# Zero products in TensorE's waits, placed by a new build-time estimate

## The chip, the cores and the metric

One core of one Trainium2 chip. The metric is device time in microseconds of one launch of the whole program; lower is better.

## The reference

Two networks one after the other, 256 latent tokens of width 1024 beside 256 context tokens, batch 1, all in float32. The first has two layers. Each applies a gated feed-forward (`swiglu`, hidden 2816), a mixer and a second feed-forward, every one behind a root-mean-square norm whose gain, shift and output gate come from a conditioning vector through a large matrix (`ada_w`). The mixer of layer 0 is a gated delta rule in both directions (8 heads of 128); that of layer 1 is windowed attention with sinks (16 heads of 64, 4 for keys and values). The second network takes the 256 latent tokens and has two layers too: each a mixer (a gated linear recurrence beside causal latent attention with rotary positions, 16 heads, mixed by gates), a layer norm, a feed-forward with a convolution of three taps over time, and a layer norm:

```
x = first_block(x, c, ctx, ...)
for l in range(2):
    x = layer_norm(ALPHA * x + mixer_sublayer(x, ...))
    x = layer_norm(ALPHA * x + conv_ffn(x, w_up[l], ..., w_down[l]))
```

## The kernel before

Activations lie transposed, features in the 128 partitions and tokens in the free dimension, as 8 blocks for width 1024. Large weights come through one queue (SyncE) in pieces of 128 x 1024 float32, in the fixed order of `pieces()` (line 209). Each float32 weight is split by `convert` and `lower` (lines 464, 482) into a high part h, rounded to TensorE's faster float32r form, and a remainder lo = w − h; activations are split in the same way. A product is then three float32r matmuls (`mm3`, line 518): high by high, high by low, low by high. Products of the first network's feed-forwards have 512 columns (context and latent tokens), those of the last 256 columns only latent tokens. Attention, norms' sums, recurrences and the delta rule use plain float32 products.

All instructions are written by one Python program at build time; nothing reorders them later. `Ker` holds a list of threads (generators), each a step of the network, with a priority. A thread yields what it needs next (`need`, line 325: tiles that must be written, free buffers, keys). `run` (line 337) picks the next thread: the first by priority whose needs are estimated to be ready by the time that TensorE gets free, else the one ready soonest. Readiness comes from an estimate: every instruction passes through `note` (line 278), which adds a cost by engine, size and type to that engine's clock (`self.clock`) and writes down when the tile is written (`self.wrote`) and read (`self.read`). All dependencies of `note` go by whole tiles. So the estimate sets the order in which every engine gets its work; each engine then runs its own list in that order and waits by semaphores.

Two more choices use the clocks. `flex` (line 402) gives a subtraction, product or sum of two SBUF operands to VectorE or to GpSimd, whichever is estimated to end first; `lower` and the second half of every split go through it. `copy` (line 409) and `affine` (line 416) choose between ScalarE and VectorE.

The places where one stage hands over to the next: `norm_half` (line 812) for the first network's norms, each half of the tokens by itself, and `layer_norm` (line 1810) for the second network. Both sum squares by products with ones (128 columns of output), take a power on GpSimd, spread the result over the partitions by a second set of products, and then normalise the eight blocks one by one on VectorE and ScalarE; `linear2` (line 537) consumes these blocks as they come, two weight pieces at a time. The delta rule's inner solve (`dn_join`, line 1238) uses many products of 16 to 64 rows.

Of the kernel before, what the change touches and what calls it, by code (L numbers as in the profile page):

```python
# [8 lines left out]
F32 = mybir.dt.float32  # L9
F32R = mybir.dt.float32r  # L10
BF16 = mybir.dt.bfloat16
I32 = mybir.dt.int32
AF = mybir.ActivationFunctionType
ALU = mybir.AluOpType
AX = mybir.AxisListType

P = 128
# [100 lines left out]
def pack_w(w):  # L118

    import numpy as np  # L120

    k, n = w.shape
    return np.ascontiguousarray(w.reshape(k // P, P, n // P, P).transpose(2, 1, 0, 3)).reshape(n // P, P, k)


def layouts(a):
# [29 lines left out]
    wo = a["dn_w_out"][0]  # L156
    we = wo[:P * EARLY, :768].reshape(EARLY // 2, 2, P, 2, 384)
    o["dn_oe"] = np.ascontiguousarray(we.transpose(3, 0, 2, 1, 4)).reshape(EARLY, P, 768)
    o["dn_ol"] = np.ascontiguousarray(wo[P * EARLY:, :768]).reshape(8 - EARLY, P, 768)
    o["dn_out"] = pack_w(wo[:, 768:])  # L160
# [48 lines left out]
def pieces():  # L209
# [7 lines left out]
    o += t("dn_in", [8 * s + h for w, h in DN_ORDER for s in {"k": (1,), "q": (0, 2), "z": (3,)}[w]])  # L217
    o += t("dn_oe", range(EARLY)) + t("dn_ol", range(8 - EARLY)) + t("dn_out", range(2))
    o += weave(w1(0, 1) + w2(0, 1), ada(0, 8) + ada(1, 0, 1, 2))
# [11 lines left out]
class Engine:  # L231
# [5 lines left out]
    def __getattr__(self, op):  # L237
        fn = getattr(self.real, op)

        def call(*a, **k):  # L240
            self.K.note(self.name, op, a, k)
            return fn(*a, **k)  # L242

        setattr(self, op, call)
        return call
# [8 lines left out]
NBLK, NRAW, NHL, NSM = 70, 5, 4, 22  # L254


class Ker:
    def __init__(self, ctx, tc, I, out):
        self.tc, self.I, self.out = tc, I, out
        self.nc = Engines(self, tc.nc)  # L260
        pool = lambda n, b, **k: ctx.enter_context(tc.tile_pool(name=n, bufs=b, **k))
        self.keep = pool("keep", 1)
        self.pools = {
            "r": (pool("raw", NRAW), NRAW), "w": (pool("hl", NHL), NHL), "b": (pool("blk", NBLK), NBLK),
            "s": (pool("sm", NSM), NSM), "p": (pool("ps", 8, space=bass.MemoryType.PSUM), 8),
        }
        self.live = {k: set() for k in self.pools}
        self.dr = pool("dr", 3, space=bass.MemoryType.DRAM)
        self.n = 0
        self.clock = {n: 0.0 for n in ("tensor", "vector", "scalar", "gpsimd", "sync", "dma")}  # L270
        self.wrote, self.read = {}, {}
        self.threads, self.done = [], set()
        self.order, self.at, self.loaded = pieces(), 0, 0
        self.dm, self.cv, self.ahead = [], [], NRAW - 2
        self.most, self.lag, self.low = NHL, False, None


    def note(self, eng, op, a, k):
        aps = [x for x in a if isinstance(x, bass.AP)]
        kin = [x for n, x in k.items() if isinstance(x, bass.AP) and n != "accum_out"]  # L280
        outs = aps[:1] + ([k["accum_out"]] if k.get("accum_out") is not None else [])
        ins = aps[1:] + kin
        o = aps[0]
        n = math.prod(o.shape[1:])
        cols = sum(1 for x in ins if math.prod(x.shape[1:]) == 1)
        if eng == "tensor":
            if op == "matmul":
                m = aps[2]
                n = math.prod(m.shape[1:])
                c = n * {F32: 1.68, BF16: 0.44}.get(m.dtype, 0.422)  # L290
                if m.dtype == F32 and o.shape[0] <= 64:
                    c *= o.shape[0] / P
            else:
                c = 109.0
        elif eng == "scalar":
            c = 75 + 0.83 * n + 93 * cols + (93 if len(outs) > 1 else 0)
        elif eng == "vector":
            fast = op in ("tensor_copy", "tensor_scalar", "memset") and not any(x.space == bass.MemoryType.PSUM for x in ins)
            c = 65 + n * (6.6 if op == "reciprocal" else 0.52 if fast else 1.04) + 60 * cols
        elif eng == "gpsimd":  # L300
            c = 60 + n * (165 if ALU.pow in a else 2.28 if op == "tensor_tensor" else 1.5)
        else:
            c = 450
        key = lambda x: x.tensor.name
        t = self.clock[eng]
        for x in ins:
            e, w = self.wrote.get(key(x), (0.0, eng))
            t = max(t, e + (200 if w != eng or eng != "tensor" else 0))
        for x in outs:
            for table in (self.wrote, self.read):  # L310
                e, w = table.get(key(x), (0.0, eng))
                if w != eng:
                    t = max(t, e + 200)
        t += c
        self.clock[eng] = t
        if eng == "sync":
            b = math.prod(o.shape) * 4
            self.clock["dma"] = t = max(self.clock["dma"], t) + b / 340
            t += 1700
        for x in ins:  # L320
            self.read[key(x)] = (max(t, self.read.get(key(x), (0.0, ""))[0]), eng)
        for x in outs:
            self.wrote[key(x)] = (t, eng)

    def need(self, *aps, b=0, p=0, s=0, when=None, e=None):

# [10 lines left out]
    def run(self):  # L337

        while self.threads:
            best = None  # L340
            for th in self.threads:
                aps, b, p, s, when, e = th[3]
                if (when and not when()) or b > self.free_of("b") or p > self.free_of("p") or s > self.free_of("s"):
                    continue
                r = max([self.wrote[x.tensor.name][0] + 200 for x in aps], default=0.0)
                if e:
                    r = max(r, self.clock[e] - SLACK)
                if best is None or r < best[0]:
                    best = (r, th)
                if r <= self.clock["tensor"]:  # L350
                    break
            assert best, ("no thread can go on", [(t[0], t[2], t[3][1:]) for t in self.threads], {k: len(v) for k, v in self.live.items()})
            th = best[1]
            try:
                th[3] = next(th[2]) or self.need()
            except StopIteration:
                self.threads.remove(th)
# [6 lines left out]
    def get(self, kind, shape, dt=F32):  # L364
        pool, n = self.pools[kind]
        assert len(self.live[kind]) < n, (kind, sorted(self.live[kind]))
        t = pool.tile(list(shape), dt, tag=kind, name=self.nm(kind))
        self.live[kind].add(t.tensor.name)
        return t

    def free(self, *tiles):
        for t in tiles:
            for s in self.live.values():
                if t.tensor.name in s:
                    s.remove(t.tensor.name)
                    break
            else:
                raise AssertionError(t.tensor.name)

    def bank(self):  # L380
        return self.get("p", (P, 512))
# [20 lines left out]
    def flex(self, n):  # L402

        now = self.clock["tensor"]
        d = max(now, self.clock["vector"]) + 65 + 1.04 * n
        g = max(now, self.clock["gpsimd"]) + 60 + 2.28 * n
        return self.nc.vector if d <= g else self.nc.gpsimd

    def copy(self, out, x):
# [54 lines left out]
    def convert(self):  # L464

        while self.free_of("w") and len(self.cv) < self.most:
            e = next((e for e in self.dm if e[0][0] != "ada"), None)
            if e is None or (self.cv and self.wrote[e[1].tensor.name][0] > self.clock["tensor"] + 1000):
                return
            self.dm.remove(e)  # L470
            key, t, n = e
            w = self.get("w", (P, 2, 1024), F32R)
            h, lo = w[:, 0], w[:, 1]
            self.copy(h[:, :n], t[:, :n])
            self.lower()
            self.low = h[:, :n], lo[:, :n], t
            if not self.lag:
                self.lower()
            self.cv.append((key, h, lo))
            self.fill()  # L480
# [123 lines left out]
    def setup(self):  # L604
        nc, I = self.nc, self.I
        keep = lambda n, shape, dt=F32: self.keep.tile(list(shape), dt, name=n)
# [3 lines left out]
        o, w = PAR_COLS["cond"]  # L610
# [18 lines left out]
        self.fill()  # L629
        self.cbf = keep("cbf", (P, 384), BF16)  # L630
        nc.sync.dma_start(self.cbf, I["cbf"])
        self.row = keep("row", (P, 48))
        nc.sync.dma_start(self.row, I["row"])
        self.sel = keep("sel", (P, 4))
# [808 lines left out]
    def deltanet(self, X, i, segs, nxt):  # L1443
# [53 lines left out]
        for g in (0, 3):  # L1497
            B = []
            for j in range(EARLY // 2):
                W = yield from self.pull("dn_oe", 0, EARLY // 6 * g + j)  # L1500
                yield self.need(p=0 if B else 3)
# [747 lines left out]


EARLY = 6
FLIGHT = 4
ROOMQ = 6
SLACK = 1000
# [39 lines left out]
```

## Time and profile before

| | us |
|---|---|
| median of 3 runs | 2867.35 (2855.65 to 2868.4) |
| the profiled execution | 2863.03 |
| its span, first to last instruction | 2861.2 |
| TensorE busy | 2741.8 (96%) |
| VectorE busy | 2160.0 (75%) |
| ScalarE busy | 910.1 (32%) |
| GpSimd busy | 675.9 (24%) |
| mean granted TensorE clock | 0.977 of full |

Busy shares are averages over the whole span. PE stands for TensorE's matmuls, PEld for its weight loads, DVE for VectorE, ACT for ScalarE, POOL for GpSimd, SP for SyncE. Because every instruction goes through one helper, almost all have the line L242; groups are told apart by tile names (p a PSUM bank, w a split weight, r a raw weight, b a block of activations, s a small tile, io the identity and ones). A matmul's duration includes its way through the array, so neighbours overlap; how fast they follow each other is read from their count in a window. [...]

### The profile page before, as it was taken

How to read it: one execution, taken by the hardware profiler on the slowest of the kernel's cores; microseconds unless marked ns; L12 is line 12 of the kernel's file. 1: busy time of each engine (PE TensorE's matmuls, PEld its weight loads, DVE VectorE, ACT ScalarE, POOL GpSimd, SP SyncE). 2: the span in 40 equal slices, each digit the busy share in tenths (PEclk: the TensorE clock that was granted, in tenths of full speed). 3: DMA queues.
4: the chain of work that ended last, by engine and by line, in shares of the span. 5: the costliest groups of instructions: out<-in, count | busy, mean ns of one | idle time of the engine just before them, and what ended most of it. 6: DMA issues, size and time to landing. Idle time of an engine off the chain costs nothing.

```text
span 2861.2 us, 47754 instructions
## 1 busy us (share of the span) xinstructions
PE 2741.8 (96%) x18916; PEld 2448.6 (86%) x18916; DVE 2160.0 (75%) x3980; ACT 910.1 (32%) x1980; POOL 675.9 (24%) x680
## 2 busy tenths in 40 slices
PE   7999999999989999999999999999899999898998
PEld 5888888888878888888888968999888999888998
DVE  5898868677756777668766578876878986878995
ACT  3111126345422110021111254214654333753432
POOL 3000335335412000120001322103513323512230
PEclk9999999999999999999999999999999999999999
DMA  7666542112223555536666213655434655334653
GB/s 268 196 186 205 182 148 78 46 39 74 61 71 114 182 154 179 152 109 200 186 209 187 79 60 93 190 179 170 144 113 142 186 174 166 116 113 132 197 171 118
DMA packets 145120, 412.59 MB, mean 144 GB/s; under 512 B 31232, under 2 KB 38144, under 8 KB 144896
## 3 DMA queue, kind: packets, MB, share of 16 engines
q1 hardware_dynamic: 144896, 409.54, 46.2%
q8 instruction: 149, 2.44, 0.4%
q14 instruction: 75, 0.61, 0.1%
HBM read 397.95 MB, written 11.53 MB: 143 GB/s over the span
## 4 chain that ended last, share of the span: by engine, by line
PE 82%; DVE 10%; issue 3%; ACT 2%; POOL 1%; DMA 1%; SPq 0%; POOLq 0%; ACTq 0%; DVEq 0%
PE p L242 82%; DVE b L242 6%; DVE w L242 3%; ACT b L242 2%; DVE s L242 1%; POOL b L242 1%; ACT w L242 1%; DMA b<-in_ada 0%; POOL w L242 0%; DMA io<-in_const 0%; DMA r<-in_w 0%; POOL s L242 0%; SPq L242 0%; ACT L242 0%; DMA b<-d 0%
## 5 line engine op out<-in xcount | busy, mean ns | idle before, releaser
L242 PE MATMUL p<-b,w 128*128 128x256 f32 (+1 forms) x14166 | 2370.0, 328 | 33.5 <-ACT b L242 12.8
L242 PEld LDWEIGHTS p<-b,w 128*128 128x128 f32 x14166 | 2093.0, 193 | 251.0 <-ACT b L242 16.6
L242 DVE TENSOR_TENSOR w<-r,w 128x1024 fp32r<-128x1024 f32 (+1 forms) x512 | 654.9, 1282 | 56.7 <-ACT w L242 44.5
L242 POOL TENSOR_TENSOR b<-b,b 128x256 fp32r<-128x256 f32 (+3 forms) x264 | 277.3, 1063 | 746.4 <-ACT b L242 555.5
L242 POOL TENSOR_TENSOR w<-r,w 128x1024 fp32r<-128x1024 f32 (+1 forms) x79 | 191.7, 2427 | 996.6 <-ACT w L242 832.9
L242 DVE CAST w<-r 128x1024 fp32r<-128x1024 f32 (+1 forms) x367 | 259.3, 707 | 183.9 <-PE p L242 149.8
L242 DVE SCALAR_TENSOR_TENSOR b<-r,b 128x512 f32<-128x512 f32 x448 | 346.2, 773 | 11.4
L242 ACT CAST b<-b 128x256 fp32r<-128x256 f32 (+1 forms) x284 | 130.7, 467 | 646.7 <-DVE b L242 560.1
L242 ACT CAST w<-r 128x1024 fp32r<-128x1024 f32 (+1 forms) x224 | 227.4, 1021 | 251.7 <-PE p L242 132.3
L242 PE MATMUL p<-b,b 128*128 128x128 f32 (+8 forms) x2872 | 270.7, 259 | 23.8 <-DVE b L242 15.7
L242 PEld LDWEIGHTS p<-b,b 32*32 32x32 f32 (+4 forms) x2872 | 211.9, 148 | 63.2 <-issue 18.9
L242 DVE TENSOR_TENSOR b<-b,b 128x256 fp32r<-128x256 f32 (+3 forms) x243 | 157.4, 654 | 120.0 <-ACT b L242 115.7
L242 ACT ACTIVATE b<-b 128x256 f32<-128x256 f32 (+1 forms) x188 | 90.8, 495 | 426.5 <-DVE b L242 404.0
L242 ACT ACTIVATE b<-p 128x128 f32<-128x128 f32 (+2 forms) x280 | 114.8, 415 | 287.9 <-PE p L242 287.6
L242 DVE TENSOR_TENSOR b<-b,p 128x256 f32<-128x256 f32 (+1 forms) x234 | 115.1, 502 | 41.2 <-PE p L242 34.9
L242 DVE SCALAR_TENSOR_TENSOR b<-p,par_t,b 128x255 f32<-128x255 f32 (+2 forms) x240 | 106.5, 475 | 16.0 <-ACT b L242 14.8
L242 PE MATMUL p<-io,b 128*128 128x128 f32 (+1 forms) x564 | 87.8, 287 | 30.7 <-POOL b L242 15.7
L242 ACT COPY b<-p 128x512 f32<-128x512 f32 (+5 forms) x161 | 71.9, 458 | 126.0 <-PE p L242 71.5
L242 PEld LDWEIGHTS p<-io,b 128*128 128x128 f32 x564 | 68.9, 167 | 42.5 <-POOL b L242 15.9
L242 POOL TENSOR_TENSOR b<-b 128x256 f32<-128x256 f32 x50 | 57.7, 1155 | 177.5 <-DVE b L242 177.5
L242 DVE SCALAR_TENSOR_TENSOR b<-p,mod,b 128x256 f32<-128x256 f32 x92 | 40.6, 478 | 68.1 <-PE p L242 68.1
L242 POOL TENSOR_TENSOR s<-s,mhalf 128x4 f32<-128x4 f32 (+2 forms) x36 | 35.6, 988 | 183.2 <-DVE s L242 182.1
(108 smaller groups left out, 1298.4 us busy)
## 6 DMA issues: line engine op xcount, KB each, us to landing
r<-in_w SPq DMA_DIRECT2D x240, 512.0 KB, 3.9
r<-in_ada SPq DMA_DIRECT2D x128, 512.0 KB, 4.2
r<-in_w_up SPq DMA_DIRECT2D x96, 512.0 KB, 3.7
r<-in_w_in SPq DMA_DIRECT2D x76, 512.0 KB, 3.8
r<-in_w_down SPq DMA_DIRECT2D x48, 512.0 KB, 3.7
r<-in_dn_in SPq DMA_DIRECT2D x33, 512.0 KB, 3.7
r<-in_w SPq DMA_DIRECT2D x32, 384.0 KB, 3.6
b<-in_ada SPq DMA_DIRECT2D x32, 256.0 KB, 5.7
```

The source lines that it names most:

```text
L242: return fn(*a, **k)
```

## The change

Three things are added or rewritten. First, `warm`, called ahead of every matmul: if the estimate says that TensorE would wait at least `IDLE` = 500 ns for the operands, and the output is 128 partitions by at least 128 columns, it issues products of a 128 x 128 tile of bfloat16 zeros with the constant table `cbf` into the same output, in number `FILL` = 75% of the wait by their own cost. They either set the output to zero before the real product overwrites it, or add zero to it. None are issued before the zero tile exists and `cbf` is estimated to be there. Second, the estimate itself: costs of each engine anew (`costs`), a lag of each engine (`LAG`) in place of 200 ns, a table of small float32 products (`ARRAY`), dependencies by part of a tile instead of whole tile, reuse of buffers (`vacate`), and a hold (`port`) that keeps VectorE and GpSimd apart for operations with two SBUF operands. Third, `flex` counts that hold, with new costs. The core of the diff:

```diff
         def call(*a, **k):
+            if op == "matmul":
+                self.K.warm(fn, a, k)
             self.K.note(self.name, op, a, k)
             return fn(*a, **k)
...
+LAG = {"tensor": 54, "vector": 33, "scalar": 33, "gpsimd": 78, "sync": 60}
+ARRAY = {(32, 32, 32): 42, (16, 32, 16): 54, (32, 32, 16): 58, (64, 64, 64): 96, (128, 64, 128): 120, (64, 128, 512): 530,
+         (96, 128, 128): 250, (96, 128, 256): 484, (128, 64, 256): 240, (128, 32, 128): 44}
...
+    def since(self, table, x, eng=None):
+        p, q, c, d = self.part(x)
+        return max((e[4] for e in table.get(x.tensor.name, ()) if e[0] < q and p < e[1] and e[2] < d and c < e[3] and e[5] != eng), default=0.0)
...
+    def costs(self, eng, op, a, k, ins, outs):
...
+            elif ins[1].dtype == BF16:
+                c = 9 + n / 2.4
+            elif ins[1].dtype == F32R:
+                c = max(110.0, 13.2 + n / 2.4)
...
+            return (c if o.shape[0] == P else c + 95), c + 85, 2 * (two or fast)
+        if eng == "gpsimd":
+            if ALU.pow in a:
+                return 355 + 160 * n, 395 + 160 * n, 1
+            if op == "tensor_tensor":
+                return 130 + 2.18 * n, 175 + 2.18 * n, 2
+            return 60 + 0.9 * n, 100 + 0.9 * n, 0
...
+    def warm(self, matmul, a, k):
+        if self.zero is None:
+            return
+        now, out = self.clock["tensor"], a[0]
+        gap = max(self.since(self.wrote, x, "tensor") + LAG["tensor"] for x in a[1:]) - now
+        full = out.shape[0] == P and len(out.shape) == 2 and out.shape[1] >= P
+        if gap < IDLE or self.ready(self.cbf) > now or not full:
+            return
+        n = min(out.shape[1], 384)
+        for _ in range(int(gap * FILL / (10 + n / 2.4))):
+            b = (out[:, :n], self.zero, self.cbf[:, :n])
+            w = {"start": k.get("start", True), "stop": k.get("start", True)}
+            self.note("tensor", "matmul", b, w)
+            matmul(*b, **w)
...
     def note(self, eng, op, a, k):
...
-            t = max(t, e + (200 if w != eng or eng != "tensor" else 0))
+            t = max(t, self.since(self.wrote, x, "tensor" if eng == "tensor" else None) + LAG[eng])
...
+        if hold:
+            t = max(t, self.port["vector" if eng == "gpsimd" else "gpsimd"] - 138)
+            if hold > 1:
+                self.port[eng] = t + d
+        self.clock[eng] = t + c
...
     def flex(self, n):
         now = self.clock["tensor"]
-        d = max(now, self.clock["vector"]) + 65 + 1.04 * n
-        g = max(now, self.clock["gpsimd"]) + 60 + 2.28 * n
+        d = max(now, self.clock["vector"], self.port["gpsimd"]) + 68 + 1.045 * n
+        g = max(now, self.clock["gpsimd"], self.port["vector"]) + 130 + 2.18 * n
         return self.nc.vector if d <= g else self.nc.gpsimd
...
         nc.sync.dma_start(self.cbf, I["cbf"])
+        self.zero = keep("zero", (P, P), BF16)
+        nc.gpsimd.memset(self.zero, 0.0)
...
+IDLE, FILL = 500, 0.75
```

## Rows read from the trace of the kernel before

**Rows 1.** The page: the span, and busy time, share and count by engine.

```profile
span 2861.2 us, 47754 instructions
PE 2741.8 (96%) x18916; PEld 2448.6 (86%) x18916; DVE 2160.0 (75%) x3980; ACT 910.1 (32%) x1980; POOL 675.9 (24%) x680
```

**Rows 2.** The page: the chain that ended last, share by engine.

```profile
PE 82%; DVE 10%; issue 3%; ACT 2%; POOL 1%; DMA 1%; SPq 0%; POOLq 0%; ACTq 0%; DVEq 0%
```

**Rows 3.** Windows of dense stages: stretch, length, engines' busy, clock, DMA share, GB/s.

```profile
100.00:120.00 20.00, 20.00 (x90) 16.58 (x89) 16.61 (x33) 3.00 (x5) 2.40 (x1) 1.00 0.51 154
1860.00:1880.00 20.00, 20.00 (x169) 20.00 (x168) 15.74 (x21) 3.16 (x8) 0.00 (x0) 1.00 0.59 185
```

**Rows 4.** TensorE's largest waits: total us, times, longest us.

```profile
PE p L242 <- DVE b L242: 32.2, 32, 3.2
PE p L242 <- ACT b L242: 26.4, 24, 2.3
PE p L242 <- POOL b L242: 21.1, 9, 14.6
```

**Rows 5.** Windows: thirteen half-clock stretches; busy PE, PEld, DVE, ACT, POOL.

```profile
2036.60:2043.40 6.80, 6.10 (x24) 5.77 (x25) 6.63 (x8) 1.32 (x2) 6.80 (x6) 0.50 0.48 162
...
2401.80:2412.10 10.30, 7.04 (x31) 6.75 (x32) 9.70 (x22) 5.04 (x11) 5.42 (x7) 0.50 0.31 103
...
2630.50:2637.30 6.80, 4.29 (x18) 3.99 (x19) 6.38 (x15) 2.93 (x7) 2.85 (x5) 0.50 0.46 154
sum 82.20, PE 64.69 PEld 60.09 DVE 68.21 ACT 32.65 POOL 38.66; mean PE 4.98 PEld 4.62 DVE 5.25 ACT 2.51 POOL 2.97
```

**Rows 6.** Windows: the other seven half-clock stretches.

```profile
504.00:514.30 10.30, 10.30 (x88) 8.32 (x87) 6.95 (x14) 4.60 (x15) 4.32 (x7) 0.50 0.37 91
...
sum 49.90, PE 38.53 PEld 32.86 DVE 30.93 ACT 21.62 POOL 19.86; mean PE 5.50 PEld 4.69 DVE 4.42 ACT 3.09 POOL 2.84
```

**Rows 7.** The chain in order of time: start us, length us, what.

```profile
407.19 5.40 PE p L242 x26
...
1240.69 358.40 PE p L242 x1665
...
2505.08 18.95 PE p L242 x115
...
2630.98 1.23 PE p L242 x4
```

**Rows 8.** Groups by form: the bfloat16 products; count, busy us, mean ns.

```profile
L242 PE MATMUL p<-cbf 128*128 128x128 bf16 x96 | 18.9, 224 | 0.0
```

**Rows 9.** Timeline of VectorE and GpSimd: start us, us, engine, operation.

```profile
399.25 2.38 POOL L242 TENSOR_TENSOR w<-r,w 128x1024 fp32r<-128x1024 f32 x1 [2.80 <-DVE w L242]
399.42 2.49 DVE L242 TENSOR_TENSOR b<-b,b 128x256 fp32r<-128x256 f32 x1
...
404.02 0.41 DVE L242 TENSOR_TENSOR b<-b,b 128x256 fp32r<-128x256 f32 x1
...
405.06 1.23 DVE L242 TENSOR_TENSOR w<-r,w 128x1024 fp32r<-128x1024 f32 x1
...
2400.61 2.34 POOL L242 TENSOR_TENSOR w<-r,w 128x1024 fp32r<-128x1024 f32 x1
2400.67 2.29 DVE L242 SCALAR_TENSOR_TENSOR s<-s 128x2 f32<-128x2 f32 x1 [0.82 <-POOL s L242]
```

**Rows 10.** VectorE's groups by form: count, busy us, mean ns.

```profile
L242 DVE TENSOR_TENSOR w<-r,w 128x1024 fp32r<-128x1024 f32 x472 | 613.2, 1302 | 49.9 <-ACT w L242 38.8
...
L242 DVE TENSOR_TENSOR b<-b,b 128x256 fp32r<-128x256 f32 x81 | 43.9, 544 | 34.3 <-ACT b L242 34.3
L242 DVE TENSOR_TENSOR b<-b,b 128x256 f32<-128x256 f32 x68 | 43.4, 657 | 22.3 <-ACT b L242 20.2 <-POOL b L242 1.7
```

**Rows 11.** Windows of the two up-projections of the second network.

```profile
2200.00:2320.00 120.00, 120.00 (x1002) 120.00 (x1001) 112.94 (x169) 50.14 (x98) 35.83 (x31) 1.00 0.61 187
2660.00:2780.00 120.00, 120.00 (x1002) 120.00 (x1001) 112.74 (x169) 47.70 (x95) 38.00 (x32) 1.00 0.62 184
```

More of the change, by code (lines that the diff above doesn't have):

```diff
@@ L267, in __init__ @@
         self.live = {k: set() for k in self.pools}
+        self.slots = {k: [(k, i) for i in range(n)] for k, (_, n) in self.pools.items()}
+        self.slot_of, self.busy = {}, {}
+        self.idle, self.used, self.step = {}, {}, 1
+        self.array, self.turn = None, 0
         self.dr = pool("dr", 3, space=bass.MemoryType.DRAM)
@@ L271, in __init__ @@
         self.wrote, self.read = {}, {}
+        self.zero = None
+        self.port = {"vector": 0.0, "gpsimd": 0.0}
         self.threads, self.done = [], set()
@@ L275, in __init__, with part, ready @@
         self.most, self.lag, self.low = NHL, False, None
+    def part(self, x):
+        pitch = x.ap[0][0]
+        p, c = divmod(x.offset, pitch) if pitch else (0, x.offset)
+        return p, p + x.ap[0][1], c, c + 1 + sum((n - 1) * step for step, n in x.ap[1:])
+    def since(self, table, x, eng=None):
+        p, q, c, d = self.part(x)
+        return max((e[4] for e in table.get(x.tensor.name, ()) if e[0] < q and p < e[1] and e[2] < d and c < e[3] and e[5] != eng), default=0.0)
+    def ready(self, x):
+        return self.since(self.wrote, x)
@@ new lines, in touch @@
+    def touch(self, table, x, t, eng):
+        p, q, c, d = self.part(x)
+        old = table.get(x.tensor.name, ())
+        table[x.tensor.name] = [e for e in old if not (p <= e[0] and e[1] <= q and c <= e[2] and e[3] <= d)] + [(p, q, c, d, t, eng)]
+    def costs(self, eng, op, a, k, ins, outs):
+        o = outs[0]
+        psum = lambda x: x.space == bass.MemoryType.PSUM
+        size = lambda x: math.prod(x.shape[1:])
+        wide = [x for x in ins if size(x) > 1 or size(o) == 1]
+        cols = len(ins) - len(wide)
+        n = max([size(o)] + [size(x) for x in wide])
+        if eng == "tensor":
+            n = size(o)
+            if op != "matmul":
+                c = 109.0 if o.shape[0] == P else 62.0
+            elif ins[1].dtype == BF16:
+                c = 9 + n / 2.4
+            elif ins[1].dtype == F32R:
+                c = max(110.0, 13.2 + n / 2.4)
+            else:
+                c = ARRAY.get((ins[0].shape[0], o.shape[0], n), max(222.0, 11 + n / 0.6))
+            part = (ins[0].shape[0], o.shape[0]) if o.shape[0] * ins[0].shape[0] <= 64 * 64 else None
+            self.turn, self.array = (95 if part != self.array else 0), part
+            return c, c + 167, 0
+        if eng == "scalar":
+            c = (50 if any(map(psum, ins)) else 98) + 0.835 * n + 92 * cols + 92 * (len(outs) > 1)
+            d = c + (110 if any(map(psum, ins)) else 95)
+            return (c if o.shape[0] == P else d + 10), d, 0
+        if eng == "vector":
+            onchip = not any(map(psum, ins + outs))
+            two = len([x for x in wide if not psum(x)]) > 1
+            fast = op in ("tensor_copy", "tensor_scalar", "memset") and onchip
+            if op == "tensor_tensor_scan":
+                c = 1080.0
+            else:
+                c = 68 + (0.525 if fast else 1.045) * n + 60 * cols + 127 * (len(outs) > 1)
+            return (c if o.shape[0] == P else c + 95), c + 85, 2 * (two or fast)
[5 more added lines that the diff above has]
+            return 60 + 0.9 * n, 100 + 0.9 * n, 0
+        return 600.0, 600.0, 0
@@ L282, in note @@
         ins = aps[1:] + kin
[L283 to L303, printed above, removed]
@@ L304, in note @@
-        key = lambda x: x.tensor.name
         t = self.clock[eng]
         for x in ins:
-            e, w = self.wrote.get(key(x), (0.0, eng))
-            t = max(t, e + (200 if w != eng or eng != "tensor" else 0))
+            t = max(t, self.since(self.wrote, x, "tensor" if eng == "tensor" else None) + LAG[eng])
         for x in outs:
[L310 to L313, printed above, removed]
@@ L314, in note @@
-        t += c
-        self.clock[eng] = t
-        if eng == "sync":
-            b = math.prod(o.shape) * 4
-            self.clock["dma"] = t = max(self.clock["dma"], t) + b / 340
-            t += 1700
+            t = max(t, self.since(self.wrote, x, eng) + LAG[eng], self.since(self.read, x, eng) + LAG[eng])
+        c, d, hold = self.costs(eng, op, a, k, ins, outs)
+        if eng == "tensor":
+            t += self.turn
+        if hold:
+            t = max(t, self.port["vector" if eng == "gpsimd" else "gpsimd"] - 138)
+            if hold > 1:
+                self.port[eng] = t + d
@@ L320, in note @@
+        self.clock[eng] = t + c
+        t += d
+        if eng == "sync":
+            b = math.prod(outs[0].shape) * 4
+            self.clock["dma"] = t = max(self.clock["dma"], t) + b / 345
+            t += 1500
+        self.step += 1
+        for x in ins + outs:
+            self.used[x.tensor.name] = self.step
         for x in ins:
-            self.read[key(x)] = (max(t, self.read.get(key(x), (0.0, ""))[0]), eng)
+            self.touch(self.read, x, t, eng)
         for x in outs:
-            self.wrote[key(x)] = (t, eng)
+            self.touch(self.wrote, x, t, eng)
@@ L344, in run @@
                     continue
-                r = max([self.wrote[x.tensor.name][0] + 200 for x in aps], default=0.0)
+                r = max([self.ready(x) + LAG["tensor"] for x in aps], default=0.0)
                 if e:
@@ L368, in get @@
         self.live[kind].add(t.tensor.name)
+        slot = min(self.slots[kind], key=lambda i: self.idle.get(i, 0))
+        self.slots[kind].remove(slot)
+        self.slot_of[t.tensor.name] = slot
+        if slot in self.busy:
+            self.read[t.tensor.name] = self.busy.pop(slot)
         return t
@@ L375, in free @@
                     s.remove(t.tensor.name)
+                    self.vacate(t.tensor.name)
                     break
@@ L378, in free, with vacate @@
                 raise AssertionError(t.tensor.name)
+    def vacate(self, name):
+        slot, busy = self.slot_of.pop(name), {}
+        self.idle[slot] = self.used.pop(name, self.step)
+        for table in (self.wrote, self.read):
+            for e in table.pop(name, ()):
+                busy[e[5]] = max(busy.get(e[5], 0.0), e[4])
+        self.busy[slot] = [(0, P, 0, 1 << 30, t, eng) for eng, t in busy.items()]
+        self.slots[slot[0]].append(slot)
     def bank(self):
@@ L467, in convert @@
             e = next((e for e in self.dm if e[0][0] != "ada"), None)
-            if e is None or (self.cv and self.wrote[e[1].tensor.name][0] > self.clock["tensor"] + 1000):
+            if e is None or (self.cv and self.ready(e[1]) > self.clock["tensor"] + 1000):
                 return
```

## The prediction, made before the run

> **What bounds the kernel now.** I read the page first. TensorE is busy 2741.8 of 2861.2 us and VectorE 2160.0 [rows 1], and 82% of the chain that ended last is matmuls, 10% VectorE work [rows 2]. So the kernel is bound by TensorE nearly throughout. In the dense stages nothing is left to take: 90 products of 512 columns in 20 us are 222 ns each, 169 of 256 columns are 118 ns each, both at granted clock 1.00 [rows 3]. The change does not touch that work, so whatever it gains must come from two things: TensorE's waits and its clock.
>
> The waits come next. TensorE's largest groups are 32.2 us behind VectorE, 26.4 behind ScalarE and 21.1 behind GpSimd, 65 waits in all [rows 4]. One of 14.6 us is the start; the rest, some 65 us, are waits of 0.5 to 3.2 us where one stage hands over to the next (norms, rotary steps, the first products on a fresh norm).
>
> Last the clock, searched in small windows. [...] Thirteen of them, 82.2 us together with 64.7 us of TensorE busy, come behind such waits ahead of wide products [rows 5]. Seven more (49.9 us, 38.5 busy) come otherwise: at the start, before narrow products of the attention, at the end, and twice, as at 504.0, in a stretch in which TensorE was busy the whole time with small products [rows 6].
>
> **The change, part by part.** Three parts matter: zero products in waits, a new estimate that sets the whole order, and the choice between VectorE and GpSimd made from it.
>
> *Clock.* Where the estimate sees a wait of at least 500 ns before a product with 128 partitions and 128 or more columns of output, it now issues bfloat16 products of zeros for 75% of it. The thirteen stretches of [rows 5] are of that kind; the seven of [rows 6] mostly are not: the start is before the table that the zeros read has come, and the outputs there are 2 columns wide, transposes or small blocks. If the thirteen ran at full clock, half of their 64.7 us of products could go: 32 us, the upper end. But products done sooner help only where TensorE is what ends last. The chain says where: laid over the thirteen, its TensorE pieces cover 42.5 us, from 4.7 us of the piece at 407.19, by all 3.4 us of the stretch inside the piece at 1240.69 and 6.0 us of the one at 2505.08, to 1.2 us of the one at 2630.98, eleven pieces in all [rows 7]. Half is 21 us. In the other 22 us the operands arrive late anyway: in the stretch from 2401.8, VectorE is busy 9.70 of 10.30 us and TensorE 7.04 [rows 5]. VectorE is close behind in several of the eleven too (6.63 of 6.80 us in the stretch from 2036.6, by its row), and not every wait will be foreseen. I take 13 us gained; bounds 0 and 32.
>
> [...]
>
> *Price of the zeros.* One product of up to 384 columns: the trace has none, but on the line through 118 ns at 256 columns and 222 ns at 512 [rows 3] it is 170 ns, between those ends at full clock and double at half clock. The only bfloat16 products in the trace, 128 columns, show 224 ns from start to end, 96 in 18.9 us [rows 8]. Some 65 us of waits at 75% make about 290 zeros, 50 us of new TensorE work. It lies in waits and costs nothing while the wait is as long as estimated; the 25% left free is the cover. If the wait is shorter, the zeros stand in TensorE's queue in front of the real product, and everything behind it waits. With one wait in three overrun by 0.2 us, the 65 waits give 4 us. Bounds: 0, and 20 us if four zeros in ten meet no wait. I take 4. The memset of the zero tile, one more operation on GpSimd during the opening transfers, is hidden by the 14.6 us wait.
>
> *Estimate and order.* The old estimate adds 200 ns to nearly every dependency and treats a tile as a whole; the new one tells parts of a tile apart, has a lag for each engine, tracks reuse of buffers, and holds VectorE and GpSimd apart where both read two operands from SBUF. All instructions may be reordered, and no row gives the price of that as such. The nearest rows are those of the collision it now models. At 399.42 a VectorE subtraction takes 2.49 us beside a GpSimd subtraction of 2.38 begun just before; the same form takes 0.41 us at 404.02. At 2400.67 a tiny VectorE step takes 2.29 us beside GpSimd's 2.34 [rows 9]. The first happens at three norms (again at 1232.2 and 1601.2), the second at three layer norms (again at 2179.5 and 2628.6), and each stands on the chain: 6 x 2.1 = 12.6 us. The new rule compares both engines with the other's hold counted in, so the weight subtraction should go to VectorE, 1.23 us [rows 9], and leave 0.9 of each 2.1: 5 us. Over the whole run VectorE's 472 weight subtractions average 1302 ns against 1.23 us, its 68 and 81 operations of 256 columns 657 and 544 ns against 0.41 [rows 9, 10]: 34 + 17 + 11 = 62 us stretched. VectorE's share of the chain, 10% of 2861 us or 286 us, is 13% of its busy time, so 8 us of the 62 lie on the path; part of them are the six again. I take 10 us for all of the reordering together, with −25 and +15 as ends: the gain of twice the six collisions, and as a loss about one more collision of 2.1 us at seven of the thirteen hand-overs, where another order could put one.
>
> *Sum.* 13 + 10 − 4 = 19 us off. The profiled execution took 2863.0 us (span 2861.2 and 1.8 around it), so 2844. Its median of three is 2867.4 with a run at 2855.7, so against the median it is 23 us, 0.8%. What can be told from no change here is about 0.5%, 14 us; the forecast is little more than that.
>
> **Rivals.**
> *The clock is not held, or hardly.* At 504.0 TensorE is busy 10.30 of 10.30 us and the clock is at half all the same [rows 6]: being busy is not what counts. Products against a tile of zeros may count as little. Against it: those were small blocks of the array, and every dense full-width stretch holds 1.00 [rows 3]. Then the zeros cost up to 8 us, double where the clock is low, and the order gives 10: 2861, no change.
>
> *The full clock loss comes back.* All 132 us at half clock go to full [rows 5, 6], also those after narrow products because the order around them differs, and every product and wait in them shrinks with the clock: half of 132, 66 us, 2797. [...] For it: nearly every stretch follows a wait; against it: VectorE's rows above, and seven stretches out of reach.
>
> *VectorE becomes the bound in the up-projections (slower).* In the two stages of some 135 us before 2329 and 2778, VectorE is busy 112.94 and 112.74 of 120 us and GpSimd 35.83 and 38.00 with 31 and 32 operations [rows 11]. GpSimd's estimate now carries a higher base price and the other engine's hold, so work moves to VectorE. All of it, at 0.41 us an operation, makes 112.9 + 12.7 = 125.7 us: 6 us over in 120, 13 over both stages. It decides once more than 17 of the 31 operations move. With the same squeeze in the norms (another 5 us), the zeros' 4 and no clock gain where VectorE sets the pace: 2885. Against it: fewer collisions shorten VectorE's own operations, by up to 62 us in the whole run.
>
> **How the numbers follow.** Forecast (2825 to 2858): 0.48. Clock not held (2850 to 2872): 0.20. Full recovery (2780 to 2825): 0.14. VectorE the bound (2870 to 2905): 0.18. The predicted time is the forecast's, 2844. The range reaches over the second rival and into both outer ones, 2800 to 2880, and leaves about 0.07 below and 0.10 above. Beyond 0.5% of the median means under 2853 or over 2882. Faster takes four fifths of the forecast, all of full recovery and a little of the second, 0.56; slower is most of the last, 0.15; the rest, 0.29, is no measurable change.
>
> **What would show it.** Right: several hundred new bfloat16 products ahead of the norms' products and the first products on a fresh norm; granted clock 1.00 in most of the thirteen stretches, while the two with small products keep half clock; the collisions of [rows 9] gone; TensorE's busy time up although the span falls. Wrong: zeros there and the clock still at half behind them; or zeros followed at once by a product whose operands had long been ready; or TensorE waiting on VectorE inside the up-projections, where it waits for nothing now. A fall of more than 40 us would mean that I undervalued the order, a rise that the new estimate misplaces work.

## The result, and the profile after

The changed kernel takes 2848.6 us (9 runs, 2846.6 to 2854.1) against 2866.0 for the kernel before on the same chip: ratio 0.9944, 95% interval 0.9926 to 0.9961, 16 us less. Measured again with the last experiments it is 0.9945 (0.9928 to 0.9961). Forecast: 2844, 0.8% less.

The page of the changed kernel, its span and busy times, to be held against [rows 1]:

```profile
span 2845.2 us, 48728 instructions
PE 2768.2 (97%) x19442; PEld 2462.2 (87%) x19442; DVE 2115.9 (74%) x4200; ACT 1012.1 (36%) x2096; POOL 237.2 (8%) x345
```

TensorE has 526 instructions more and is busy 26 us longer in a span 16 us shorter. GpSimd lost two thirds of its work. VectorE does 220 operations more and is busy 44 us less. One reason is that casts of weights went from it to ScalarE, 95 of them. Here are VectorE's casts, before and after (count, then busy us and mean ns):

```profile
L242 DVE CAST w<-r 128x1024 fp32r<-128x1024 f32 (+1 forms) x367 | 259.3, 707 | 183.9 <-PE p L242 149.8
L244 DVE CAST w<-r 128x1024 fp32r<-128x1024 f32 (+1 forms) x272 | 186.4, 685 | 183.2 <-PE p L244 162.7
```

The groups by form show the other; they answer to [rows 8] and [rows 10]:

```profile
L244 DVE TENSOR_TENSOR w<-r,w 128x1024 fp32r<-128x1024 f32 x531 | 650.4, 1229 | 107.3 <-ACT w L244 99.6
L244 DVE TENSOR_TENSOR b<-b,b 128x256 fp32r<-128x256 f32 x190 | 77.7, 419 | 11.7 <-ACT b L244 11.7
L244 DVE TENSOR_TENSOR b<-b,b 128x256 f32<-128x256 f32 x140 | 59.9, 445 | 22.4 <-ACT b L244 19.2 <-POOL b L244 1.7
...
L368 PE MATMUL p<-cbf,zero 128*128 128x256 bf16 x233 | 30.1, 273 | 0.0
...
L368 PE MATMUL p<-cbf,zero 128*128 128x128 bf16 x262 | 16.6, 219 | 0.0
...
L368 PE MATMUL p<-cbf,zero 128*128 128x384 bf16 x31 | 7.7, 393 | 0.0
```

The means of VectorE's three groups fell from 1302, 544 and 657 ns to 1229, 419 and 445, close to the 1.23 and 0.41 us of [rows 9]: hardly any of them is stretched beside a GpSimd operation now. The zeros are 526 products of 54 us. TensorE's largest groups of waits come to less in total than in [rows 4], though the longest behind VectorE is now 3.9 us instead of 3.2 (33 are behind ScalarE, but none over 1.6 us; the 12.7 us is the start):

```profile
PE p L244 <- DVE b L244: 21.9, 26, 3.9
PE p L244 <- ACT b L244: 18.1, 33, 1.6
PE p L244 <- DMA b<-in_ada: 13.4, 2, 12.7
```

The windows that were searched for half clock give ten stretches, 55.7 us instead of 132. Shown are one that begins in small products, the two at the DeltaNet's end, the only one in the second network in which TensorE has work, and the sum (busy PE, PEld, DVE, ACT, POOL, then the clock):

```profile
526.60:536.90 10.30, 10.30 (x91) 8.39 (x89) 5.99 (x17) 2.91 (x6) 0.00 (x0) 0.50 0.06 14
...
823.60:830.40 6.80, 5.66 (x35) 5.50 (x36) 3.66 (x8) 0.37 (x1) 0.00 (x0) 0.50 0.07 30
840.60:847.50 6.90, 5.79 (x18) 3.87 (x19) 2.23 (x4) 1.31 (x2) 0.33 (x1) 0.51 0.00 1
2042.10:2045.60 3.50, 3.50 (x18) 3.50 (x19) 3.50 (x6) 0.00 (x0) 0.00 (x0) 0.51 0.57 178
...
sum 55.70, PE 45.20 PEld 39.09 DVE 35.61 ACT 16.68 POOL 0.85; mean PE 4.52 PEld 3.91 DVE 3.56 ACT 1.67 POOL 0.08
```

Most of the thirteen stretches of [rows 5] are gone. One that begins in small products keeps half clock, as in [rows 6]. Its products in the timeline (start us, length us; the row of 70 is four products of 128 columns and 66 of 32 x 16):

```profile
523.13 1.89 PE L244 MATMUL p<-b 16*32 16x16 f32 x64
...
525.44 3.96 PE L244 MATMUL p<-b,b 128*128 128x128 f32 x70
...
529.06 1.63 PE L244 MATMUL p<-b,w 128*128 128x512 f32 x3
...
531.90 5.30 PE L244 MATMUL p<-b,w 128*128 128x512 f32 x12
```

The clock falls at 526.60 among the products of 32 x 16, without a wait of TensorE; more than half of the stretch is then wide weight products at half clock: the twelve of 512 columns in the last row take 5.30 us, 442 ns each, where [rows 3] has 222 at full clock. At a layer norm the collision of [rows 9] is gone, and zeros stand in the wait. The timeline:

```profile
2170.24 0.71 POOL L244 TENSOR_TENSOR s<-s,mhalf 128x2 f32<-128x2 f32 x1 [4.00 <-DVE s L244]
2170.97 0.16 DVE L244 SCALAR_TENSOR_TENSOR s<-s 128x2 f32<-128x2 f32 x1 [0.82 <-POOL s L244]
...
2170.99 1.16 PE L244 MATMUL p<-io,s 128*128 128x128 f32 x8 [0.42 <-POOL s L244]
2171.05 2.35 DVE L244 TENSOR_TENSOR w<-r,w 128x1024 fp32r<-128x1024 f32 x2
2171.99 2.46 PE L368 MATMUL p<-cbf,zero 128*128 128x256 bf16 x21
```

The tiny VectorE step takes 0.16 us instead of 2.29, both weight subtractions now run on VectorE behind it, and 21 zeros cover 2.46 us of TensorE's wait; 0.87 us of it stay free behind them.

### The profile page after: what moved, and what is told of

The parts are those of the page before. It is cut to its first block, busy times and chain, and to the rows that moved or that the text cites. A ratio compares the mean times of both kernels' runs of the same rounds, so it can differ in the third digit from the quotient of the medians.

```text
span 2845.2 us, 48728 instructions
## 1 busy us (share of the span) xinstructions
PE 2768.2 (97%) x19442; PEld 2462.2 (87%) x19442; DVE 2115.9 (74%) x4200; ACT 1012.1 (36%) x2096; POOL 237.2 (8%) x345
## 5 line engine op out<-in xcount | busy, mean ns | idle before, releaser
L244 DVE TENSOR_TENSOR w<-r,w 128x1024 fp32r<-128x1024 f32 (+1 forms) x583 | 703.8, 1211 | 114.4 <-ACT w L244 105.0
L244 ACT CAST w<-r 128x1024 fp32r<-128x1024 f32 (+1 forms) x319 | 327.3, 1030 | 345.1 <-PE p L244 256.2
L244 DVE CAST w<-r 128x1024 fp32r<-128x1024 f32 (+1 forms) x272 | 186.4, 685 | 183.2 <-PE p L244 162.7
L244 DVE TENSOR_TENSOR b<-b,b 128x256 fp32r<-128x256 f32 (+3 forms) x454 | 224.5, 505 | 94.0 <-ACT b L244 88.8
L244 PE MATMUL p<-b,b 128*128 128x128 f32 (+9 forms) x2872 | 272.5, 261 | 18.8 <-DVE b L244 9.9
L244 PEld LDWEIGHTS p<-b,b 32*32 32x32 f32 (+5 forms) x2872 | 214.5, 150 | 59.3 <-ACT b L244 19.6
L244 POOL TENSOR_TENSOR b<-b,b 128x512 f32<-128x512 f32 (+2 forms) x53 | 69.6, 1313 | 1885.9 <-ACT b L244 1276.9
L244 DVE SCALAR_TENSOR_TENSOR b<-p,par_t,b 128x254 f32<-128x254 f32 (+2 forms) x240 | 110.1, 477 | 5.9 <-ACT b L244 4.7
L244 PEld LDWEIGHTS p<-io,b 128*128 128x128 f32 x564 | 66.4, 162 | 26.0 <-ACT b L244 10.9
L244 ACT ACTIVATE b<-p,par_t 128x256 f32<-128x256 f32 (+1 forms) x124 | 68.0, 551 | 5.9 <-PE p L244 5.9
L244 DVE SCALAR_TENSOR_TENSOR b<-p,cw,b 128x508 f32<-128x508 f32 (+1 forms) x96 | 68.7, 738 | 0.2
```

## The experiments

All ratios are to the kernel before, measured on the same chip. A difference between two of them is good to about 0.002, 6 us; 1 us is 0.00035.

**What each part brings.** Three switches: the new estimate, the new choice between VectorE and GpSimd, the zeros.

```diff
-IDLE, FILL = 500, 0.75
+IDLE, FILL = 1e9, 0.75          # no zeros
```

> The new estimate with no zero product at all. Theory A (my sum: zeros net 13 - 4 = 9 us, order and engine choice the rest of the 17): 8 to 10 us slower than the changed kernel, 2858, and the half-clock stretches of the second network are back, some 100 us of half clock in all. Rival B (the whole gain is the clock): the time of the kernel before, 2866. Rival C (the whole gain is the new order): 2849, whatever the clock does.

Measured 0.9966 (0.9952 to 0.9980): 10 us faster than before, so zeros bring the other 6 us, which is just what such a difference is good to. Mean clock of its runs 0.981. Apart from the zeros, every engine has the same operations in the same order here as in the changed kernel (kind, tile name and shape, one by one in the traces), so the zeros are all that differs. The same holds for the kernels below with small zeros and with zeros in one part.

```diff
-        d = max(now, self.clock["vector"], self.port["gpsimd"]) + 68 + 1.045 * n
-        g = max(now, self.clock["gpsimd"], self.port["vector"]) + 130 + 2.18 * n
+        d = max(now, self.clock["vector"]) + 65 + 1.04 * n
+        g = max(now, self.clock["gpsimd"]) + 60 + 2.28 * n
```

> The changed kernel with the old rule of choice between VectorE and GpSimd (no hold, old prices). Theory A: the collisions of VectorE with GpSimd come back, GpSimd's busy time rises from 237 us towards 676, and 5 to 8 us are lost: 2855. Rival D (the choice is worth nothing, the gain is zeros and order): 2849 with the collisions back beside other work.

Measured 1.0014 (0.9999 to 1.0030): not 6 us are lost without the new choice but 20, more than the whole gain. The edit takes out the hold and puts back the old prices; which of the two moves the work was not tried apart. With both edits, no zeros and the old choice:

> The new estimate without zeros and with the old rule of choice: what the order alone is worth. Theory A: within 3 us of the kernel before, 2866, since the DeltaNet stage got later by the new order and others earlier. Rival C: most of the 17 us, 2852. If the new costs only pay together with the rule of choice, slower than before, 2870.

Measured 1.0030 (1.0016 to 1.0045): the new order alone is 9 us slower than the old. So the 16 us are +9 for the order, −18 for the choice (1.0030 to 0.9966), −6 for the zeros. "Order" here takes in what the new clocks do to `copy` and `affine`: ScalarE is busy 1007 us in it instead of 910. The last two kernels, too, differ by zeros alone, and there they bring 5 us (1.0030 to 1.0014). What the new choice is worth in the old order was not tried. The page and the groups of this kernel (order only) show the collisions back, means of 1284 and 665 ns:

```profile
PE 2748.7 (96%) x18916; PEld 2452.2 (85%) x18916; DVE 2115.6 (74%) x3832; ACT 1007.5 (35%) x2090; POOL 760.3 (26%) x719
...
L244 DVE TENSOR_TENSOR w<-r,w 128x1024 fp32r<-128x1024 f32 x445 | 570.1, 1284 | 121.4 <-ACT w L244 113.5
L244 DVE TENSOR_TENSOR b<-b,b 128x256 fp32r<-128x256 f32 x69 | 45.3, 665 | 12.3 <-ACT b L244 11.6
```

In the two profiled executions its loss lies in the DeltaNet stage. Windows of that stage in the order-only kernel, then in the kernel before, cut where nearly the same count of weight products is done: 540 us against 526, at clock 0.93 against 0.96. Half of 75 us at half clock against half of 44 makes up the difference (an estimate: the 442 and 222 ns above say that weight products take twice as long at half clock). That is one execution of each, and the stage takes from 523 to 529 us in three executions with the same instructions up to its end (the changed kernel twice, and the one below with zeros in the first part only).

```profile
403.00:943.00 540.00, 510.15 (x4389) 441.73 (x4388) 388.54 (x811) 213.28 (x621) 189.00 (x302) 0.93 0.23 67
```

```profile
400.00:926.00 526.00, 498.91 (x4395) 431.34 (x4394) 379.17 (x792) 216.58 (x624) 213.28 (x321) 0.96 0.24 69
```

**Do the zeros need the new estimate?** The kernel before with the zero tile, the call and the same rule of 500 ns and 75%, the wait taken from the old clocks:

```diff
+        def at(x):
+            e, w = self.wrote.get(x.tensor.name, (0.0, "tensor"))
+            return 0.0 if w == "tensor" else e + 200
+        gap = max(at(x) for x in a[1:]) - now
```

> The kernel before with zero products placed by its old estimate (rule, 500 ns and 75% as in the change). Theory A: 9 us faster than before, 2857, most stretches at full clock. B: 2849, the full gain. C: 2866, no gain. A fourth possibility, that only the new estimate can place zeros: the old one adds 200 ns to each dependency, sees waits that are shorter or absent in truth, and the zeros delay products: 2866 or above though the clock is held.

Measured 1.0038 (1.0021 to 1.0055): 11 us slower, although the clock rose to 0.987. The fourth possibility holds. Windows of the zeros alone (busy, count), the old estimate first, then the changed kernel:

```profile
400.00:620.00 220.00, 11.40 (x164) 0.98 0.22 62
620.00:815.00 195.00, 11.57 (x158) 0.96 0.22 62
```

```profile
400.00:620.00 220.00, 2.51 (x34) 0.95 0.22 62
620.00:815.00 195.00, 1.32 (x6) 0.99 0.23 66
```

The other operations are those of the kernel before, in its order. The old estimate sees more waits in the DeltaNet stage than there are: its zeros take 23 us between 400 and 815 us, where TensorE of the kernel before stands idle for 10.0 and 4.6 us:

```profile
400.00:620.00 220.00, 209.96 (x1985) 0.96 0.22 62
620.00:815.00 195.00, 190.38 (x1872) 0.96 0.24 66
```

One place in the timeline of the kernel with zeros by the old estimate:

```profile
758.76 1.89 PE L244 MATMUL p<-b,b 32*32 32x16 f32 x64
...
759.50 0.34 DVE L244 SCALAR_TENSOR_TENSOR b<-p,s,b 128x128 f32<-128x128 f32 x1
760.59 0.95 PE L297 MATMUL p<-cbf,zero 128*128 128x128 bf16 x14
...
761.38 0.66 PE L244 MATMUL p<-b,b 128*128 128x128 f32 x4
```

VectorE was done at 759.84, before TensorE's small products were; 14 zeros then kept the state products behind them waiting for 0.8 us. Leaving those zeros out, and nothing else:

```diff
-        if self.zero is None:
+        if self.zero is None or self.order.index(("dn_in", 0, 8)) < self.at <= self.order.index(("dn_out", 0, 1)):
             return
```

> Zeros placed by the old estimate as in the second run, but none while the DeltaNet stage issues (422 of its 776 lay between 400 and 930 us, where TensorE waits for little). If those misplaced zeros are what made it 11 us slower: faster than before by what zeros bring elsewhere, 2855 to 2860. If the old estimate misplaces zeros everywhere: still slower than before, 2868 or more.

Measured 0.9987 (0.9969 to 1.0005): 15 us of the loss are gone, what is left is a gain of 4 us that its interval does not tell from none. Why the old estimate sees those waits I had put down to the small products, counted at 13 ns or less there and at 42 to 58 by the new costs; in the timeline above 64 of them take 1.89 us, 30 ns each:

```diff
+                if m.dtype == F32:
+                    c = ARRAY.get((aps[1].shape[0], o.shape[0], n), max(222.0, 11 + n / 0.6))
+                    part = (aps[1].shape[0], o.shape[0]) if o.shape[0] * aps[1].shape[0] <= 64 * 64 else None
+                    c += 95 if part != self.array else 0
```

> Zeros with the old estimate, of which only the costs of TensorE's float32 products are the new ones (small blocks and 95 ns on a change of block). In the run with the wholly old estimate 322 zeros (23 us of TensorE) stood between 400 and 815 us, where TensorE waits for nearly nothing. If they cost its 12 us, and came because small products were counted at 13 ns instead of 42 to 58: few zeros remain there, and 2859 or less, no slower than the kernel before. If zeros lose elsewhere, by the 200 ns that are added to each dependency: still 2870.

Measured 1.0091 (1.0065 to 1.0117), 26 us slower, with still 280 zeros between 400 and 815 us. A miss: these costs are not the reason, or not the only one, and changing them upset the order besides. Which part of the old estimate makes up the waits stays open.

**What a zero costs and what the clock gives.** The same zeros cut to a 32 x 32 block of the array:

```diff
-            b = (out[:, :n], self.zero, self.cbf[:, :n])
+            b = (out[:32, :n], self.zero[:32, :32], self.cbf[:32, :n])
```

> The changed kernel with each zero product cut to a block of 32 rows by 32 columns of the array, the same number of columns streamed: the same time in TensorE's queue, little of the array at work. If what counts for the clock is that the queue is busy, the clock stays as in the changed kernel (0.990) and the time too, 2848. If the width of the array counts, the half-clock stretches come back; then the time shows what zeros cost by themselves: 2855, that of the kernel without zeros, if they hide in waits, and 2859 if they cost the 4 us of my sum.

Measured 0.9991 (0.9976 to 1.0005), 13 us slower than with full-width zeros, clock 0.984 against 0.990. So nearly the same time in TensorE's queue (56.2 us of zeros against 54.4; 21 of 256 columns take 2.46 us in either form) went with a clock higher by 0.003 than the 0.981 without zeros, not by 0.009. Nor are these zeros free: 7 us slower than without any (whether changes between small and full blocks cost some of it was not measured). Twice as many:

```diff
-IDLE, FILL = 500, 0.75
+IDLE, FILL = 500, 1.5
```

> The changed kernel with zeros for 150% of each estimated wait instead of 75%: every filled wait is overrun by half if the estimate is exact. Waits filled now come to some 50 us, so 25 us of zeros would stand before products that are ready: up to 2870 if TensorE is what ends last behind all of them, 2855 or so if, as the chain of the kernel before said, that holds for half of them. No change (2850) would mean that the zeros lie in time that VectorE sets, whatever their number.

Measured 0.9974 (0.9961 to 0.9987): 8 us slower than the changed kernel for 29 us more of zeros (83.6 instead of 54.4), at the same clock, 0.991. With so many zeros in the estimate one operation went from ScalarE to VectorE and part of these two engines' work has another order, so not the zeros alone differ here.

Then the place. Progress curves of single executions (the time at which each share of the weight products was done) seemed to say that zeros bring 11 us up to the norm behind the DeltaNet and nothing after. Two kernels for it:

```diff
-        if self.zero is None:
+        if self.zero is None or self.at > self.order.index(("w1", 0, 1, 8)):      # first part only; <= for the second
             return
```

> Zeros only up to the first third of the feed-forward behind the DeltaNet, none later. Progress curves say that zeros brought about 11 us before that point and nothing after it, though they brought back the clock there too. If so: the time of the changed kernel, 2848, while ten half-clock stretches of the later stages return. If the clock is worth as much in each stretch (my sum): 2853.

> The opposite: zeros only behind that point. If they bring nothing there, the time of the kernel without zeros, 2855, at a mean clock well above it (0.99 against 0.979 over the later stages). If each stretch is worth its share: 2850.

Measured 0.9965 (0.9950 to 0.9979) for the first part only, that of no zeros, and 0.9948 (0.9931 to 0.9966) for the second part only, that of the changed kernel. Both point the other way, though the two intervals overlap. One execution differs from the next of the same program by up to 20 us, more than what the curves were to show.

That spread was the best measurement. Within each of 13 sets of runs (the changed kernel twice and the others here once, 130 runs), the time of a run follows its mean granted clock, correlation −0.89: 22 us less for 0.01 more of clock. The kernel before alone gives 23 in 35 runs on one chip, and 26 and 28 in 26 and 23 runs on another. If everything took twice as long at half clock, as the weight products do (442 ns against 222), 0.01 of mean clock would be 0.01 of the span, 28 us, by estimate; the slopes are four fifths of that or more. This is a correlation: a longer wait in a run costs time and may itself go with a lower clock, and no experiment set the clock alone. With 2225 us per unit of clock and one fitted price, 28% of the zeros' own time, the runs come out as follows, against the kernel without zeros (clock 0.981):

| zeros | their time, us | mean clock | worked out, us | measured, us |
|---|---|---|---|---|
| as changed (two measurements) | 54.4 | 0.9904 | −21 + 15 = −6 | −6 |
| 32 x 32 blocks | 56.2 | 0.9838 | −6 + 16 = +9 | +7 |
| 150% | 83.6 | 0.9911 | −23 + 23 = 0 | +2 |
| first part | 14.3 | 0.9827 | −4 + 4 = 0 | 0 |
| second part | 39.5 | 0.9881 | −16 + 11 = −5 | −5 |

Each measured figure is good to about 6 us, and the 28% is fitted to these five, so the table fits and does not prove; with the slopes of 26 to 28 us the price comes out at a third. Three more pairs differ in zeros alone and were not used for the fit. In the new order with the old choice (66.4 us of zeros, clock 0.9745 to 0.9862) it works out −26 + 19 = −7 us, measured −5. In the kernel before, zeros of the old estimate outside the DeltaNet stage (42.4 us, 0.9783 to 0.9848) make −14 + 12 = −2, measured −4; all its zeros (75.0 us, 0.9788 to 0.9865) make −17 + 21 = +4, measured +11, so zeros where there is no wait seem to cost more. The slope does not rest on the fit.

**Old order with new zeros.** Since the new order alone loses in the DeltaNet stage, I let threads be picked there by the old estimate, kept up beside the new one:

```diff
+            early = self.at <= self.order.index(("dn_oe", 0, 5))
+            clock = self.clock_old if early else self.clock
...
+                if early:
+                    r = max([self.wrote_old[x.tensor.name][0] + 200 for x in aps], default=0.0)
```

> The changed kernel, its threads picked by the old estimate until the last piece of the DeltaNet's early output weights, by the new one after that; zeros and engine choice by the new one throughout. By the runs the new order alone loses 12 us, all before 930 us. If that order is what loses: 8 to 10 us faster than the changed kernel, 2839. If the old order only suited the old engine choice, or zeros are misplaced in it: 2848 or slower.

Measured 1.0175 (1.0154 to 1.0196), 50 us slower than before, 66 slower than the changed kernel. A clear miss: in its execution the stage took 594 us, at half clock for over 100. Two estimates that pull at one program, one for the order and one for engines and zeros, are worse here than either alone; what in it loses I did not find.

> The changed kernel once more on the same chip as the others of this call, to compare them directly: 2848, a ratio of 0.994 to the kernel before.

Measured 0.9945 (0.9928 to 0.9961), as told above. No version tried is faster than the changed kernel.

## Why the prediction was right

*The sum* said 13 + 10 − 4 = 19 us, measured 16. The net of zeros was put at 9 and is 6; order and choice were put at 10 and are 10 (0.9966). The total held, in part by luck: the clock's term was some 8 us too small and the price of the zeros some 11, and the two nearly cancel, as loss and gain do within the third term.

*Clock, 13 us.* Too small. It rose from 0.979 to 0.990; by the slope the zeros' share, 0.981 to 0.990, is worth 21 us (an estimate, as the slope is a correlation). That is about the half of 42.5 us that the chain's pieces in [rows 7] gave and that I then cut for VectorE. The runs show 22 to 28 us for 0.01 of clock, where everything at half speed would be 28 by the estimate above: a microsecond at half clock cost closer to its half than I made it.

*Price of the zeros, 4 us.* Too small by the same table, some 15 of 54 us by the fit. Their time was foreseen well (50 us); the number was not, 526 instead of 290, as half of them have 128 columns. What failed is the cover: I let a third of the waits be overrun by 0.2 us. The traces of the changed kernel and of the one without zeros, which differ in nothing else, show it wait by wait. The zeros stand in 45 places; in 11 of them, 7.0 us of zeros, TensorE does not wait at all when they are left out, and over all 45 the zeros and the waits left beside them come to 10.7 us more than the waits without zeros. Zeros beyond those cost 8 us for 29 us more at the same clock (the doubled ones).

*Order and choice, 10 us.* Right only as a sum. Order alone loses 9 us, where I gave 15 as the end of a loss; the choice wins 18, where I gave 25 as the end of a gain. The step with the collisions named the mechanism and the right rows, but counted only those on the chain. Most of the 18 us shows as clock again (0.9745 to 0.9809, 14 us by the slope). Behind a collision TensorE waits, and in the kernel before half clock began at 2401.8 in the wait behind the collision of 2400.67 (TensorE waits 1.62 us there for VectorE, until 2403.02). In the profiles without zeros, all listed waits of TensorE come to 112 us with the old choice and 100 with the new. That the waits take the clock in the same way at every collision is argued, not shown. The order's loss of 9 us, too, is what the slope makes of its clock (0.9788 to 0.9745, 10 us).

*Rivals.* The clock not held: refuted (0.990), though the 32 x 32 zeros speak for its premise that being busy alone is not what counts (56.2 us of them gave 0.984, 54.4 us of full-width ones 0.990). The row that I took it from was misread: in the stretch from 504.0 TensorE was not at small products the whole time. Of these there are 64, 3.03 us, and twelve weight products of 512 columns follow at half clock:

```profile
505.85 3.03 PE L242 MATMUL p<-b,b 32*32 32x16 f32 x64
...
508.81 5.49 PE L242 MATMUL p<-b,w 128*128 128x512 f32 x12
```

Full recovery: no, 56 us of half clock stay. VectorE the bound: its condition came true and its conclusion did not. All of GpSimd's work in the two up-projections moved away, as the windows show, to be held against [rows 11]:

```profile
2190.00:2310.00 120.00, 120.00 (x1002) 120.00 (x1001) 98.07 (x170) 77.13 (x126) 0.00 (x0) 1.00 0.63 189
2640.00:2760.00 120.00, 120.00 (x1003) 120.00 (x1002) 98.12 (x168) 76.41 (x127) 0.00 (x0) 1.00 0.62 184
```

VectorE is busy 98 of 120 us instead of 113, with as many operations as before: in place of GpSimd's 31 in the first stage, its 30 casts of weights left for ScalarE (126 operations of 77 us there instead of 98 of 50). The new choice is not what sent them there. The order-only kernel, with the old choice, has ScalarE at 77 us as well, GpSimd at 44 and VectorE at 91 and 89:

```profile
2190.00:2310.00 120.00, 117.42 (x954) 116.46 (x955) 90.99 (x138) 77.42 (x129) 44.02 (x40) 0.98 0.55 180
2650.00:2770.00 120.00, 118.09 (x978) 117.36 (x978) 89.48 (x131) 77.46 (x127) 44.14 (x39) 1.00 0.58 184
```

So the new estimate freed VectorE, and the new choice then filled it up again, by less than it was freed. I had priced the work that arrives and not what leaves for the third engine.

## What to carry to other kernels

Before filling TensorE's waits, look for what makes it wait: here the choice of engine for two-operand work, made with the stretching of VectorE beside GpSimd counted in (means that fell from 1302, 544 and 657 ns to 1229, 419 and 445), was worth three times as much as the zeros (18 us and 6). The fillers needed an estimate that knows where TensorE truly waits; placed by a coarse one they raised the clock (0.979 to 0.987) and still lost 11 us. Compare kernels over many runs and read the mean clock beside the time: a progress curve of one execution told me the wrong place.

## What the runs showed of the hardware that I had not expected

Runs of one unchanged program range over 20 us (2855 to 2875 for the kernel before on one chip), and its mean granted clock over 0.974 to 0.983 with them, at a correlation of −0.89. The clock fell to half at 526.60 us among products of 16 x 16 and 32 x 16, though TensorE was busy without a gap from 522 on (4.60 of the 4.60 us before; the rows of the result above). And zeros in 32 x 32 blocks went with a smaller rise of the clock (0.981 to 0.984 for 56.2 us of them) than full-width ones (to 0.990 for 54.4 us), though both multiply by zero.
